# Splitting w_down into two parts with an accumulating DMA in place of a subtraction

## The chip, the cores and the metric

The kernel runs on one core of a Trainium2 chip. The time is the device time of one execution in microseconds (us). It is given as the median of three executions; one further execution was taken with the profiler, and every row quoted below is from that one.

## What is computed

Two layers of a hybrid block over a stream x (512 tokens, 1024 channels) and, in layer 0 alone, a context stream (256 tokens). What bears on the change is the feed-forward part at each layer's end:

```
D_FF = int(math.ceil(8 * D_MODEL / 3 / 128)) * 128      # 2816 = 22 blocks of 128
def conv_ffn(h, w_up, w_c, b_c, w_down):
    u = dwconv3(h @ w_up, w_c, b_c)
    gate, val = jnp.split(u, 2, axis=-1)
    return (jax.nn.silu(gate) * val) @ w_down
...
    yx = conv_ffn(fx, w_up[i], w_ffn_conv[i], b_ffn_conv[i], w_down[i])
    x = x + ga2 * rmsnorm(yx, g_post_ffn[i])
    if not last:
        yc = conv_ffn(fc, w_up[i], w_ffn_conv[i], b_ffn_conv[i], w_down[i])
```

## The kernel before

All products are made from rounded operands (fp32r). To keep fp32 accuracy each operand is split in two: a high part h, which is the value rounded to fp32r, and a low part, which is the value minus h. A product is then three matmuls (`mm3`, lines 196 to 198): high times high, high times low, low times high.

`load_w` fetches a block of 128 x 1024 weights (512 KB) into a tile Wr through SyncE's queue (line 189), and `split` makes the parts: ScalarE copies Wr to Wh, which rounds it (line 181), and VectorE or GpSimd writes Wl = Wr - Wh (line 182).

`ffn_down` needs one block of w_down for each of the 22 blocks m of D_FF. It is called for a group of two m at a time (the last call of the x stream has four) and multiplies the activations of the group before: gT for x, gc for the context. So w_down is loaded and split three times in all: for the context of layer 0 in `ffn_c` (22 blocks, split on GpSimd, since `CE` is True), for x of layer 0 in `ffn_x` (22, on VectorE) and for x of layer 1 (22, on VectorE). That makes 66 blocks.

In `ffn_x` the first half of the feed-forward product is a Strassen-like scheme of seven products for each m. Three more pairs of parts are made there for each m from w_up: from the raw block r, and from two tiles tt, which GpSimd makes with four subtractions (lines 1276 to 1279). A fourth, smaller pair is the tile w.

What sets the order:
- The pools. `BUFS` gives two buffers to Wr, four to Wh and four to Wl, and w_up and w_down share these. A new high or low part can only be written when the matmuls that read the old one in the same buffer are done.
- The scheduler. The build orders the instructions of each engine by a timeline of its own and by priority, which is the order of the code. The list so made is fixed; an engine then takes its instructions strictly in that order, and each waits for its own semaphores.
- The queues. SyncE issues all weight loads, GpSimd issues the DMAs of tables and spilled tiles, and both in their order.

Of the kernel before, what the change touches and what calls it, by code (L numbers as in the profile page):

```python
# [8 lines left out]
F32 = mybir.dt.float32  # L9
F32R = mybir.dt.float32r  # L10
I32 = mybir.dt.int32
AF = mybir.ActivationFunctionType
ALU = mybir.AluOpType
# [4 lines left out]
P = 128  # L18
# [50 lines left out]
class Net:  # L69
# [115 lines left out]
    def load_w(self, src, shape=None, el=None, tag=None, raw=None):  # L185
        shape = shape or [P, 1024]
        r = self.tl(shape, F32, raw or tag or "Wr")
        for i, a in enumerate(src if isinstance(src, list) else [src]):
            self.nc.sync.dma_start(r[:, 2 * i : 2 * i + 2] if isinstance(src, list) else r, a)
        h, lo = self.tl(shape, F32R, tag or "Wh"), self.tl(shape, F32R, tag or "Wl")  # L190
        self.split(h, lo, r, el)
        return h, lo

    def mm3(self, ps, l, r, first, last, **kw):
# [970 lines left out]
    def ffn_down(self, l, st, g, ms, begin, el=None, early=0, mid=None):  # L1165

        nc = self.nc
        end = ms[-1] == MF - 1
        if begin and st is self.X:
            st.y = [self.M("y", F32) for _ in range(st.NT)]  # L1170
        wd = {k: self.load_w(self.I["w_down"][l, k], el=nc.gpsimd if el else None) for k in ms}
        if end:
            ss = [self.small("ss", 2, 6) for _ in range(st.NT)]
            xr = [self.load_r(self.src[st.name][t]) for t in range(st.NT)]
        acc = {}

        def add(t, h, ks):
            hs, ts = slice(h * 512, (h + 1) * 512), slice(t * P, (t + 1) * P)
            if (t, h) not in acc:
                if h == 0:  # L1180
                    acc[t] = self.pw()
                acc[t, h] = acc[t][:, hs]
            for k in ks:
                self.mm3(acc[t, h], (g[k][:, 0, ts], g[k][:, 1, ts]), (wd[k][0][:, hs], wd[k][1][:, hs]), k == ms[0], k == ms[-1])
            yield 3 * len(ks) * C512, 0.0

        for t in range(early):
            for h in range(2):
                yield from add(t, h, ms[:-1])
        for t in range(st.NT):  # L1190
            y = st.y[t]
            for h in range(2):
                hs = slice(h * 512, (h + 1) * 512)
                yield from add(t, h, ms[-1:] if t < early else ms)
                if end:
                    nc.vector.tensor_tensor(y[:, hs], y[:, hs], acc[t, h], op=ALU.add)
                    self.sumsq_half(ss[t], y[:, hs], h)
                    nc.gpsimd.tensor_tensor(y[:, hs], y[:, hs], st.G[1][:, hs], op=ALU.mult)
            if begin:
                nc.scalar.copy(y, acc[t])  # L1200
            elif not end:
                nc.vector.tensor_tensor(y, y, acc[t], op=ALU.add)  # L1202
            else:
                self.tail(st, t, xr[t], ss[t])
                if t == Z["MT"] and mid:
                    yield from mid
# [495 lines left out]
```

## Time and profile before

| | before |
|---|---|
| median of three runs | 1789.37 us (1785.97 to 1790.05) |
| the profiled execution | 1784.91 us, of it 1783.1 us span |
| mean granted TensorE clock in it | 0.971 |
| context feed-forward, layer 0 | about 484 to 690 us of the span |
| x feed-forward, layer 0 | about 690 to 1092 us |
| x feed-forward, layer 1 | about 1420 to 1783 us |
| TensorE busy over the span | 1639.1 us, 92% |
| VectorE, ScalarE, GpSimd busy | 1440.1, 934.9, 692.3 us |

How to read it: the span runs from the first to the last instruction, and 1.8 us of the execution lie around it. PE is TensorE's matmul row, PEld its weight loads, DVE VectorE, ACT ScalarE, POOL GpSimd, SP SyncE. A busy PE does not mean a PE at its peak, since matmuls are pipelined; so the text also uses the pace at which matmuls start. The time of a DMA is that from the start of its issue to its landing.

### The profile page before, as it was taken

What the parts mean: (1) busy time and instruction counts of PE and PEld (TensorE: products, weight loads), DVE (VectorE), ACT (ScalarE), POOL (GpSimd) and SP (SyncE); (2) the same over time, 40 slices, a digit from 0 to 9 for tenths busy, and PEclk for the clock granted to TensorE, in tenths of its full rate; (3) what the DMA queues carried; (4) which work ended last, traced back from release to release, by engine and by line L of the source; (5) the groups of instructions that cost most, each with busy time, mean ns of one, the idle gap of its engine ahead of it and who ended that gap; (6) DMA issues with size and microseconds to landing.
All of it is one profiled execution on the core that took longest, in us unless ns stands there. A gap on an engine that the chain in (4) does not pass through costs nothing. (4 is left out here: it accounts for less than half of the span.)

```text
span 1783.1 us, 27842 instructions
## 1 busy us (share of the span) xinstructions
PE 1639.1 (92%) x10502; PEld 1397.4 (78%) x10502; DVE 1440.1 (81%) x2324; ACT 934.9 (52%) x1737; POOL 692.3 (39%) x515
## 2 busy tenths in 40 slices
PE   5799987899999997989999998998898799999997
PEld 2677775687788897878989885787787678889996
DVE  5888777697665688889988987668895878999997
ACT  2642344487565454556554556434773465555454
POOL 3343332000134337665554645212002455655543
PEclk9899999999999998999999999999999899999999
DMA  9214277603477642332342258653012343332323
GB/s 366 101 61 146 86 243 263 232 13 130 162 253 232 228 155 71 96 118 84 101 148 84 89 185 305 213 175 118 1 48 83 130 146 103 95 107 86 127 62 119
DMA packets 70003, 248.01 MB, mean 139 GB/s; under 512 B 8111, under 2 KB 9647, under 8 KB 69868
## 3 DMA queue, kind: packets, MB, share of 16 engines
q1 hardware_dynamic: 60716, 215.54, 35.6%
q0 software_dynamic: 9152, 30.68, 5.5%
q8 instruction: 83, 1.36, 0.3%
q14 instruction: 52, 0.43, 0.1%
HBM read 232.03 MB, written 14.16 MB: 138 GB/s over the span
## 5 line engine op out<-in xcount | busy, mean ns | idle before, releaser
L196 PE MATMUL pn<-h,Wh 128*128 128x256 f32 x1328 | 376.6, 286 | 11.7 <-DVE ft L638 4.3
L198 PE MATMUL pn<-h,Wl 128*128 128x256 f32 x1328 | 372.8, 284 | 10.2 <-DVE Wl L182 10.2
L197 PE MATMUL pn<-h,Wh 128*128 128x256 f32 x1328 | 374.2, 283 | 1.7 <-POOL h L182 1.7
L196 PEld LDWEIGHTS pn<-h,Wh 128*128 128x128 f32 x1328 | 253.2, 191 | 24.5 <-issue 7.8
L198 PEld LDWEIGHTS pn<-h,Wl 128*128 128x128 f32 x1328 | 252.1, 191 | 15.3 <-DVE Wl L182 12.7
L197 PEld LDWEIGHTS pn<-h,Wh 128*128 128x128 f32 x1328 | 253.8, 191 | 6.2 <-POOL h L182 2.4
L181 ACT CAST Wh<-Wr 128x1024 fp32r<-128x1024 f32 x118 | 122.7, 1049 | 138.9 <-PE pw L198 46.4
L182 DVE TENSOR_TENSOR Wl<-Wr,Wh 128x1024 fp32r<-128x1024 f32 x89 | 129.7, 1465 | 53.7 <-ACT Wh L181 53.2
L1276 POOL TENSOR_TENSOR tt<-r,r 128x512 f32<-128x512 f32 x44 | 75.0, 1705 | 233.9 <-DMA r<-w_up 211.0
L196 PE MATMUL pw<-Wh,gT 128*128 128x512 f32 x352 | 137.5, 404 | 9.0 <-ACT gT L181 3.9
L197 PE MATMUL pw<-Wl,gT 128*128 128x512 f32 x352 | 138.5, 396 | 3.1 <-DVE Wl L182 3.1
L198 PE MATMUL pw<-Wh,gT 128*128 128x512 f32 x352 | 137.8, 396 | 1.8 <-DVE gT L182 1.8
L181 ACT CAST Wh<-tt 128x1024 fp32r<-128x1024 f32 x88 | 90.8, 1048 | 84.9 <-PE pn L197 42.4
L182 DVE TENSOR_TENSOR Wl<-tt,Wh 128x1024 fp32r<-128x1024 f32 x88 | 122.5, 1411 | 11.0 <-ACT Wh L181 8.0
L1335 POOL TENSOR_TENSOR ft<-ft,ft 128x512 f32<-128x512 f32 x44 | 70.8, 1609 | 132.4 <-DVE ft L638 94.2
L1202 DVE TENSOR_TENSOR y<-y,pw 128x1024 f32<-128x1024 f32 x82 | 99.2, 1213 | 20.1 <-PE pw L198 20.0
L182 POOL TENSOR_TENSOR h<-tf,h 128x256 fp32r<-128x256 f32 (+1 forms) x40 | 36.0, 921 | 187.8 <-ACT h L181 186.5
L182 POOL TENSOR_TENSOR Wl<-Wr,Wh 128x1024 fp32r<-128x1024 f32 x29 | 74.6, 2578 | 57.7 <-ACT Wh L181 56.5
L1278 POOL TENSOR_TENSOR tt<-r,tt 128x512 f32<-128x512 f32 x44 | 75.8, 1722 | 51.9 <-DVE Wl L182 51.9
L196 PE MATMUL pw<-h,Wh 128*128 128x256 f32 (+1 forms) x224 | 76.9, 343 | 13.9 <-DVE v L638 2.6
L283 PE MATMUL pn<-wm,cpad 128*32 128x256 f32 x768 | 67.6, 411 | 19.7 <-DMA wm<-w_mod 19.3
L636 ACT ACTIVATE ft<-C,vec 128x512 f32<-128x512 f32 x88 | 68.7, 811 | 32.1 <-DVE C L1325 25.7
(361 smaller groups left out, 4706.1 us busy)
## 6 DMA issues: line engine op xcount, KB each, us to landing
wm<-w_mod SPq DMA_DIRECT2D x96, 512.0 KB, 5.4
r<-w_up SPq DMA_DIRECT2D x90, 512.0 KB, 3.6
Wr<-w_down SPq DMA_DIRECT2D x66, 512.0 KB, 3.8
L<-w_up SPq DMA_DIRECT2D x44, 512.0 KB, 4.4
Wr<-w_out SPq DMA_DIRECT2D x24, 512.0 KB, 3.6
Wr<-w_in_t SPq DMA_DIRECT2D x16, 512.0 KB, 3.9
dft<-hdft_x POOLq DMA_DIRECT2D x16, 512.0 KB, 4.1
Wr<-w_in_c SPq DMA_DIRECT2D x12, 512.0 KB, 3.6
```

Of the source, the lines that this page charges most:

```text
L181: r = nc.scalar.copy(hi, src)
L182: (el or nc.vector).tensor_tensor(lo, src, f32(hi), op=ALU.subtract)
L196: nc.tensor.matmul(ps, l[0], r[0], start=first, stop=False, **kw)
L197: nc.tensor.matmul(ps, l[0], r[1], start=False, stop=False, **kw)
L198: nc.tensor.matmul(ps, l[1], r[0], start=False, stop=last, **kw)
L283: nc.tensor.matmul(ps[32 * g : 32 * g + 32, cs], self.cpad[:, q % 2 * 4 + g, :], w[:, g, :], start=q % 2 == 0, stop=q % 2 == 1, skip_group ...
L636: nc.scalar.activation(dst, ps, AF.Identity, scale=w1, bias=b)
L1202: nc.vector.tensor_tensor(y, y, acc[t], op=ALU.add)
L1276: te.tensor_tensor(half(t13, 0), half(r[1], 0), half(r[0], 0), op=ALU.subtract)
L1278: te.tensor_tensor(half(t24, 0), half(r[1], 1), half(t13, 0), op=ALU.subtract)
L1335: nc.gpsimd.tensor_tensor(o[0], o[0], o[1], op=ALU.mult)
```

## The change

For w_down alone, `load_w` gives way to a new function. It still loads Wr through SyncE's queue and still copies Wr to Wh on ScalarE. The low tile is first filled by ScalarE with the negated Wr, rounded to fp32r, which is the negated high part. Then a DMA issued by GpSimd reads the same block of w_down from HBM a second time and adds it to what stands in Wl. The subtraction goes, on both engines, in all 66 blocks.

```diff
+    def load_w_acc(self, src):
+        nc = self.nc
+        r = self.tl([P, 1024], F32, "Wr")
+        nc.sync.dma_start(r, src)
+        h, lo = self.tl([P, 1024], F32R, "Wh"), self.tl([P, 1024], F32R, "Wl")
+        nc.scalar.activation(lo, r, AF.Copy, scale=-1.0)
+        nc.scalar.copy(h, r)
+        nc.gpsimd.dma_start(lo, src, accum_op=ALU.add)
+        return h, lo
...
-        wd = {k: self.load_w(self.I["w_down"][l, k], el=nc.gpsimd if el else None) for k in ms}
+        wd = {k: self.load_w_acc(self.I["w_down"][l, k]) for k in ms}
```

In the new code the copies stand in lines 200 (the negated one) and 201 (Wh) and the accumulating DMA in line 202; all later lines have moved by 11, so `mm3` is in lines 207 to 209, GpSimd's four subtractions in 1287 to 1290, and the multiplication of line 1335 in 1346.

The scheduler has laid the instructions out anew from the first w_down block on. One group of two blocks in the middle of layer 1's x feed-forward serves as the example. The first place is ScalarE. Before, the two roundings of w_down have one activation of the convolution between them:

```order
L1298 COPY C_15830<-pn_15831 128x256
L181 CAST Wh_15764<-Wr_15762 128x1024
L636 ACTIVATE ft_15749<-C_15626,vec_101 128x512
L181 CAST Wh_15770<-Wr_15768 128x1024
L181 CAST gT_15621<-ft_15613 128x512
```

Now four full passes over a block follow each other, and in each pair the high part comes ahead of the negated one, though the code has them the other way round:

```order
L1309 COPY C_15882<-pn_15883 128x256
L201 CAST Wh_15814<-Wr_15812 128x1024
L200 ACTIVATE Wl_15815<-Wr_15812 128x1024
L201 CAST Wh_15821<-Wr_15819 128x1024
L200 ACTIVATE Wl_15822<-Wr_15819 128x1024
L647 ACTIVATE ft_15799<-C_15676,vec_101 128x512
```

What moved: the convolution's activation stands behind all four passes, and the accumulating DMA of the first block has two passes ahead of it.

The second place is GpSimd's queue at the same group. Before, it holds only the four subtractions for the next m and the multiplications:

```order
L1276 TENSOR_TENSOR tt_15936<-r_15929,r_15928 128x512
L1277 TENSOR_TENSOR tt_15936<-r_15929 128x512
L1335 TENSOR_TENSOR ft_15613<-ft_15613,ft_15614 128x512
L1278 TENSOR_TENSOR tt_15937<-r_15929,tt_15936 128x512
L1279 TENSOR_TENSOR tt_15937<-tt_15937,r_15928 128x512
L1335 TENSOR_TENSOR ft_15749<-ft_15749,ft_15750 128x512
```

Now the two accumulating DMAs stand behind the four subtractions and ahead of a multiplication:

```order
L1288 TENSOR_TENSOR tt_15988<-r_15981 128x512
L1289 TENSOR_TENSOR tt_15989<-r_15981,tt_15988 128x512
L1290 TENSOR_TENSOR tt_15989<-tt_15989,r_15980 128x512
L202 DMA Wl_15815<-w_down 128x1024
L202 DMA Wl_15822<-w_down 128x1024
L1346 TENSOR_TENSOR ft_15799<-ft_15799,ft_15800 128x512
```

What moved: two DMA issues are new here, and each waits for ScalarE's negated copy with the multiplication queued behind it.

The third place is TensorE's first use of the low part. Before (Wl_15765):

```order
L198 MATMUL pn_15860<-h_14318,Wl_15741 128x256
L196 MATMUL pn_15860<-h_14318,Wh_15740 128x256
L197 MATMUL pw_15774<-Wl_15765,gT_15417 128x512
L198 MATMUL pw_15774<-Wh_15764,gT_15417 128x512
L197 MATMUL pw_15788<-Wl_15765,gT_15417 128x512
```

Now (Wl_15815):

```order
L208 MATMUL pn_15926<-h_14370,Wh_15788 128x256
L209 MATMUL pn_15926<-h_14369,Wl_15789 128x256
L208 MATMUL pw_15826<-Wl_15815,gT_15465 128x512
L209 MATMUL pw_15826<-Wh_15814,gT_15465 128x512
L207 MATMUL pw_15826<-Wh_15821,gT_15671 128x512
L208 MATMUL pw_15840<-Wl_15815,gT_15465 128x512
```

What moved: little. Between the last matmul that reads the old content of this buffer and the first that reads the new low part, there stand 40 matmuls of 256 columns and 2 of 512 columns; before, there were 44 and 2 at this group, and 38 and 2 at most groups of the layer. The first use of the second block's low part stands later than before: 10 us of matmuls behind the release of its buffer, against 6.

## The prediction

> **What bounds the kernel now.** I read first the busy time by stage (the view of windows), then TensorE's waits in the two x feed-forward stages, where 44 of the 66 blocks are split.
>
> ```profile
> core 0: us, PE busy (x) PEld busy (x) DVE busy (x) ACT busy (x) POOL busy (x), PEclk, DMA share, GB/s
> 484.00:690.00 206.00, 200.13 (x1457) 177.28 (x1456) 151.87 (x234) 111.21 (x173) 92.19 (x57) 0.98 0.61 205
> 690.00:1092.00 402.00, 379.40 (x2540) 340.59 (x2538) 348.70 (x440) 217.71 (x357) 223.57 (x144) 0.98 0.38 126
> 1420.00:1745.00 325.00, 314.17 (x2180) 287.39 (x2180) 290.60 (x319) 173.87 (x270) 169.70 (x103) 0.99 0.32 104
> ...
> PE pn L198 <- DVE Wl L182: 4.5, 6, 1.4
> PE pw L197 <- DVE Wl L182: 3.1, 2, 2.0
> PE pw L196 <- DVE y L1202: 2.6, 1, 2.6
> ...
> PE pw L198 <- DVE gT L182: 0.9, 1, 0.9
> ...
> PE pn L198 <- DVE Wl L182: 4.1, 3, 2.5
> ...
> PE pn L196 <- DVE C L1323: 1.1, 3, 0.7
> PE pw L198 <- DVE gT L182: 0.9, 1, 0.9
> ...
> PE pw L196 <- DVE y L1202: 0.7, 2, 0.4
> ```
>
> The three stages are bound by TensorE: it is busy 200 of 206, 379 of 402 and 314 of 325 us. VectorE, at 87 and 89%, is near, but not the bound. All of TensorE's idle time in the two x stages is 22.6 + 10.8 = 33.4 us. The rows of waits (the first four those of 690 to 1092 us, the rest those of 1420 to 1745) lay 11.1 + 6.8 = 17.9 us of it to VectorE, and only 3.1 us (pw L197) to a low part of the down product. That is all that a lighter VectorE can give back.
>
> **What is removed.** The subtractions: 22 blocks in each x stage on VectorE, and the context's on GpSimd.
>
> ```profile
> L182 DVE TENSOR_TENSOR Wl<-Wr,Wh 128x1024 fp32r<-128x1024 f32 x22 | 36.7, 1677 | 2.9 <-ACT Wh L181 2.9
> L182 DVE TENSOR_TENSOR Wl<-Wr,Wh 128x1024 fp32r<-128x1024 f32 x22 | 36.9, 1697 | 0.5 <-ACT Wh L181 0.4
> L182 POOL TENSOR_TENSOR Wl<-Wr,Wh 128x1024 fp32r<-128x1024 f32 x20 | 51.3, 2573 | 46.7 <-ACT Wh L181 46.5
> ```
>
> VectorE loses 73.6 us of work, GpSimd 51.3. Nearly all of it lies beside matmuls. Of the 17.9 us I credit a third, 6 us: the waits on gT, C and y are for work with other inputs, and only a part of them stems from VectorE's queue being full. In the context stage I credit nothing: TensorE waits there on no GpSimd row, and is 97% busy.
>
> **What is added.** 66 passes of ScalarE, 66 DMA issues on GpSimd, and 66 times 512 KB through the DMA engines.
>
> ```profile
> L181 ACT CAST Wh<-Wr 128x1024 fp32r<-128x1024 f32 x118 | 122.7, 1049 | 138.9 <-PE pw L198 46.4
> L716 POOL DMA_DIRECT2D dft<-hdft_x x16: 527/591/956, 79.7 to 1173.0; - x16
> Wr<-w_down SPq DMA_DIRECT2D x66, 512.0 KB, 3.8
> dft<-hdft_x POOLq DMA_DIRECT2D x16, 512.0 KB, 4.1
> DMA to landing us min/median/max: 8.3/11.1/14.1
> GB/s 13 16 203 340 258 307 311 332 392 410 416 419 416 419 383 400 410 416 406 397 410 413 419 419 410 89 92 318 279 292 367 272 288 200 13 190 275 56 301 416
> ```
>
> As work this is cheap: 66 x 1.05 = 69 us for a ScalarE that is about half busy in these stages (217.71 of 402), 66 x 0.59 = 39 us for GpSimd, less than it loses, and 34.6 MB for DMA engines that are at most 61% busy. Its cost is latency. A low part was ready one ScalarE pass and one subtraction after its buffer came free; now it takes two passes, an issue and a landing, and TensorE's order leaves no more room for that. Here is one group in the timeline before:
>
> ```profile
> 1547.62 1.06 ACT L181 CAST Wh<-Wr 128x1024 fp32r<-128x1024 f32 x1
> 1550.04 1.65 DVE L182 TENSOR_TENSOR Wl<-Wr,Wh 128x1024 fp32r<-128x1024 f32 x1
> 1551.71 4.27 SPq L189 DMA_DIRECT2D Wr<-w_down  x2
> 1552.06 0.28 PE L196 MATMUL pn<-h,Wh 128*128 128x256 f32 x1
> 1552.18 0.28 PE L197 MATMUL pn<-h,Wh 128*128 128x256 f32 x1
> 1552.89 0.40 PE L197 MATMUL pw<-Wl,gT 128*128 128x512 f32 x1
> 1553.12 0.40 PE L198 MATMUL pw<-Wh,gT 128*128 128x512 f32 x1
> 1542.47 2.17 POOL L1279 TENSOR_TENSOR tt<-tt,r 128x512 f32<-128x512 f32 x1
> 1548.36 2.24 POOL L1276 TENSOR_TENSOR tt<-r,r 128x512 f32<-128x512 f32 x1 [3.72 <-DVE Wl L182]
> ```
>
> ScalarE starts at 1547.6, as soon as the old matmuls are done; the subtraction ends at 1551.7, and TensorE reads the low part at 1552.9: 1.2 us to spare, no stall. Matmuls start every 0.118 us (256 columns, the rows of 1552.06 and 1552.18) or 0.235 us (512). In the new order 40 short and 2 long ones lie between the release and the first use: 40 x 0.118 + 2 x 0.235 = 5.2 us. Into this must go about 0.2 us to ScalarE's start, two passes of 1.05, 0.1 to the issue (both small times are my estimates from rows like these), and the landing time A of an accumulating DMA. So TensorE stalls A - 2.8 us in such a group.
>
> **The price of A.** No row shows an accumulating DMA. Lower bound: a plain 512 KB copy issued by GpSimd lands in 4.1 us. Far end: the rows "to landing" of h<-spill_h, GpSimd's four fp32-to-fp32r copies of 512 KB beside other loads, give 8.3 us for the fastest and 11.1 for the median. I take 4.1 plus two transfers of 512 KB at the 419 GB/s of a full slice, 1.25 us each: one because the old content of Wl has to be read as well, one because the negated copy that releases this DMA also frees Wr, so that SyncE's next load starts at the same moment (in the timeline it starts at 1551.71, where the subtraction ends). A = 6.6 us, nearer to the plain copy since only two transfers collide, not eight. The far ends stay for the range.
>
> In the Trainium skill, the page Collectives: The Full Stack, section "Why ReduceScatter is half of AllGather", says that the add in a DMA engine costs no time itself, but that it needs two source reads on one ring, which halves the rate. By that alone A would be 4.1 + 1.25 = 5.35 us and the stalls would add up to 35 us; no row here shows it.
>
> **The sum.** The room between a buffer's release and its first use, counted in the new order for each group and turned into time with the two paces, gives at A = 6.6: ten groups with 5.2 us of room (three at the end of layer 0, seven in layer 1) at 3.7, 37 us; one in layer 1 with 6.1 us, 2.8; one in layer 0 whose two blocks have only 2.8 and 6.3 us, 9.3 together; the other groups of the x stages, with 7 to 9 us, 9 in all; and nothing for layer 0's last four blocks (15 us and more) or the context's (10 to 19). That is 58 us. The second block of a group has 10 us of room and needs 2.1 us more than the first: no stall of its own. At A = 4.1 the same sum is 17 us, at 8.3 it is 111, at 11.1 it is 239.
>
> What is queued behind the new waits: on GpSimd the two issues wait for ScalarE until about 5 us after the release, and the multiplication L1346 stands behind them. Its result gT is first read a group (31 us of matmuls) later, so this costs nothing. ScalarE's two activations of the convolution are pushed back some 4 us; TensorE's next need of their banks falls in its own stall. GpSimd's four subtractions stand ahead of the issues and run at 1.3 to 2.2 us each; if they end late, A starts late, and this is part of why the range leans upward. Since every stall stands on TensorE, the bound, it goes fully into the time.
>
> Net: 58 - 6 = +52 us. The profiled execution, 1784.9, would become 1837. It lay 4.5 us under the median of the three runs, so against the median the forecast is 1789.4 + 52 = 1841 us. One measurement of this kernel can tell 0.2% (3.6 us) from no change.
>
> **Rivals.**
> 1. The accumulating DMA lands like a plain one, A = 4.1 (the row of dft speaks for it, the doubled read against it): 17 - 6 = +11, 1800 us. Chance 0.15.
> 2. VectorE's relief wins. If A is 3.8, as SyncE's w_down loads have it, the ten groups stall 0.9 us each and the others 4, 13 us, and if all 17.9 us of waits on VectorE went, the kernel would end at 1785; some more, since freed tt tiles let GpSimd start earlier, at 1775 to 1785. It decides below A of about 4.2. For it: VectorE is nearly 90% busy. Against it: TensorE waits little on it. Faster 0.11; no change within 0.2%, with A near 4, 0.09.
> 3. The add is much slower than a copy, or GpSimd's subtractions hold the issue back by 2 us and more: A of 8.3 and above, +105 us, 1894 us or more. For it: the slow h<-spill_h. Against it: those ran at full DMA load. Chance 0.17.
>
> The forecast itself, A between 4.5 and 8, has 0.48. So slower by over 0.2%: 0.48 + 0.15 + 0.17 = 0.80; same 0.09; faster 0.11. For 8 in 10 the range starts below rival 1 (1796) and ends at rival 3's near edge (1894).
>
> In the Trainium skill, DMA: Bandwidth & Descriptors, section "Issuing engines are not separate DMA queues", has DMAs of all issuing engines on the same 16 engines; the 11.1 us of h<-spill_h at full load agree. By it a move to GpSimd's queue alone buys no bandwidth.
>
> **What would show it.** The row of the accumulating DMAs should show 5.5 to 8 us to landing. TensorE's waits should have a new row at the down product (pw, the line of high times low, now 208) that waits for a DMA or for Wl, with ten and more waits of 2.5 to 5 us; VectorE should be 70 us less busy, ScalarE 69 us more, and the context stage as long as before. The prediction is wrong if A is about 4 us or less, if the stalls appear in the context stage too (then ScalarE or GpSimd's order is the cause), or if TensorE's idle time falls.

## The result, and the profile after

| | before | after |
|---|---|---|
| median | 1788.56 us (4 runs, 1785.97 to 1790.05) | 1940.65 us (4 runs, 1931.73 to 1948.43) |
| ratio | | 1.085, 95% interval 1.080 to 1.0901 |
| profiled span | 1783.1 us | 1936.4 us |
| mean granted TensorE clock | 0.971 | 0.931 |

The change costs 152 us. The forecast was +52 us with a range up to 1894, so it had the sign right, but the size is almost three times as large.

The first view is the busy time by stage, with the stages' new bounds:

```profile
core 0: us, PE busy (x) PEld busy (x) DVE busy (x) ACT busy (x) POOL busy (x), PEclk, DMA share, GB/s
484.00:705.00 221.00, 203.54 (x1456) 179.72 (x1455) 144.83 (x235) 130.19 (x196) 48.67 (x52) 0.98 0.80 241
705.00:1160.00 455.00, 389.52 (x2502) 350.02 (x2500) 310.78 (x389) 233.57 (x360) 222.55 (x165) 0.91 0.46 129
1507.00:1936.00 429.00, 365.59 (x2310) 328.91 (x2310) 283.62 (x350) 210.39 (x323) 197.75 (x135) 0.90 0.42 118
```

The third stage before, taken to its end like the one above:

```profile
1420.00:1783.00 363.00, 340.95 (x2307) 308.25 (x2306) 316.39 (x371) 187.78 (x300) 183.38 (x113) 0.98 0.32 106
```

TensorE is idle for 17, 65 and 63 us of these stages. Before, it was idle for 6, 23 and 22 us. The granted clock, 0.98 in both x stages before, is 0.91 and 0.90. VectorE got lighter, as the change meant it to, and that bought nothing. The waits of TensorE have one large new row. The first row below is that of the whole span; the three behind it are those of the context, of x in layer 0 and of x in layer 1. The columns are us in total, times, and the longest.

```profile
PE pw L208 <- DMA Wl<-w_down: 104.7, 31, 7.7
...
PE pw L208 <- DMA Wl<-w_down: 13.0, 8, 2.5
...
PE pw L208 <- DMA Wl<-w_down: 44.7, 12, 7.7
...
PE pw L208 <- DMA Wl<-w_down: 47.1, 11, 6.4
```

One group of layer 1 in the timeline (start, duration, engine) shows the mechanism:

```profile
1653.75 1.05 ACT L201 CAST Wh<-Wr 128x1024 fp32r<-128x1024 f32 x1 [1.62 <-PE pn L208]
1654.71 1.05 ACT L200 ACTIVATE Wl<-Wr 128x1024 fp32r<-128x1024 f32 x1
...
1656.11 0.88 POOL L202 DMA_DIRECT2D Wl<-w_down  x1
...
1655.79 2.23 SPq L198 DMA_DIRECT2D Wr<-w_down  x2
...
1658.73 0.28 PE L209 MATMUL pn<-h,Wl 128*128 128x256 f32 x1
1663.36 0.79 PE L208 MATMUL pw<-Wl,gT 128*128 128x512 f32 x1 [4.35 <-DMA Wl<-w_down]
...
1666.09 0.41 PE L207 MATMUL pn<-h,Wh 128*128 128x256 f32 x1
1666.30 0.41 PE L208 MATMUL pn<-h,Wh 128*128 128x256 f32 x1
...
1668.34 0.28 PE L208 MATMUL pn<-h,Wh 128*128 128x256 f32 x1
1668.46 0.28 PE L209 MATMUL pn<-h,Wl 128*128 128x256 f32 x1
```

Up to 1663.36 this is the forecast, step by step, with a somewhat longer stall than the 3.7 us of the sum. ScalarE starts at 1653.75 and makes two passes, SyncE's next load starts at the moment the negated copy ends, GpSimd issues at 1656.11, and 7.25 us later TensorE goes on, after a stall of 4.35 us. But look at the four matmuls behind the stall. Those at 1666.09 and 1666.30 start 0.21 us apart, and the same kind at 1668.34 and 1668.46 starts 0.12 us apart. The view of windows shows why (ahead of the stall, behind it, and later; the third number from the end is the granted clock):

```profile
1630.00:1661.00 31.00, 29.01 (x202) 26.88 (x201) 24.74 (x29) 17.34 (x26) 16.90 (x11) 0.99 0.30 81
1661.50:1668.00 6.50, 4.64 (x15) 4.06 (x16) 0.82 (x1) 1.14 (x2) 1.94 (x1) 0.50 0.88 246
1668.50:1690.00 21.50, 21.50 (x146) 19.66 (x145) 19.75 (x21) 10.00 (x15) 11.52 (x7) 1.00 0.25 74
```

The stall is followed by several us at a granted clock of 0.50. That term is not in my sum at all. Short stalls cost less of it: in the context stage, where the longest wait is 2.5 us, the mean clock stays at 0.98.

How the 152 us divide was worked out from the starts of the three-part matmuls (8100 in the whole run, some 6700 of them from the context stage's first low part on, which are those used). An interval of more than 2.3 times the pace at full clock is counted as a stall; what a shorter one has over that pace is counted as slow pace. Stalls went from 236.6 to 350.6 us (+114), slow pace from 29.3 to 65.6 us (+36).

### The profile page after: what moved, and what is told of

It reads as the page before. It is cut to its first block, busy times and chain, and to the rows that moved or that the text cites. A ratio compares the mean times of both kernels' runs of the same rounds, so it can differ in the third digit from the quotient of the medians.

```text
span 1936.4 us, 27997 instructions
## 1 busy us (share of the span) xinstructions
PE 1692.3 (87%) x10502; PEld 1440.3 (74%) x10502; DVE 1371.8 (71%) x2280; ACT 997.7 (52%) x1803; POOL 667.4 (34%) x559
## 5 line engine op out<-in xcount | busy, mean ns | idle before, releaser
L207 PE MATMUL pn<-h,Wh 128*128 128x256 f32 x1328 | 385.0, 293 | 13.8 <-ACT Wh L181 8.2
L208 PE MATMUL pn<-h,Wh 128*128 128x256 f32 x1328 | 381.8, 290 | 1.9 <-POOL h L182 1.9
L207 PEld LDWEIGHTS pn<-h,Wh 128*128 128x128 f32 x1328 | 264.1, 199 | 26.4 <-ACT Wh L181 11.4
L208 PEld LDWEIGHTS pn<-h,Wh 128*128 128x128 f32 x1328 | 264.1, 199 | 6.9 <-POOL h L182 2.5
L208 PE MATMUL pw<-Wl,gT 128*128 128x512 f32 x352 | 151.7, 431 | 87.2 <-DMA Wl<-w_down 87.2
L207 PE MATMUL pw<-Wh,gT 128*128 128x512 f32 x352 | 147.3, 428 | 5.2 <-ACT Wh L201 2.9
L208 PEld LDWEIGHTS pw<-Wl,gT 128*128 128x128 f32 x352 | 71.1, 202 | 107.5 <-DMA Wl<-w_down 93.1
L209 PE MATMUL pw<-Wh,gT 128*128 128x512 f32 x352 | 147.6, 420 | 0.0
L182 DVE TENSOR_TENSOR Wl<-tt,Wh 128x1024 fp32r<-128x1024 f32 x88 | 131.0, 1506 | 16.1 <-ACT Wh L181 16.0
L648 DVE SCALAR_TENSOR_TENSOR ft<-C,vec,ft 128x511 f32<-128x511 f32 x88 | 89.9, 1049 | 54.7 <-ACT ft L647 54.7
L1213 DVE TENSOR_TENSOR y<-y,pw 128x1024 f32<-128x1024 f32 x82 | 99.4, 1213 | 39.3 <-PE pw L209 39.2
L202 POOL DMA_DIRECT2D Wl<-w_down x66 | 60.3, 920 | 136.2 <-ACT Wl L200 88.6
L181 ACT CAST Wh<-Wr 128x1024 fp32r<-128x1024 f32 x52 | 54.3, 1050 | 86.7 <-PE pw L209 45.4
L182 DVE TENSOR_TENSOR Wl<-Wr,Wh 128x1024 fp32r<-128x1024 f32 x45 | 56.1, 1249 | 51.7 <-ACT Wh L181 51.4
```

Of the source, the lines that this page charges most:

```text
L181: r = nc.scalar.copy(hi, src)
L182: (el or nc.vector).tensor_tensor(lo, src, f32(hi), op=ALU.subtract)
L202: nc.gpsimd.dma_start(lo, src, accum_op=ALU.add)
L207: nc.tensor.matmul(ps, l[0], r[0], start=first, stop=False, **kw)
L208: nc.tensor.matmul(ps, l[0], r[1], start=False, stop=False, **kw)
L209: nc.tensor.matmul(ps, l[1], r[0], start=False, stop=last, **kw)
```

## The experiments

All times are medians; ratios are to the kernel before, run on the same chip, with a 95% interval. Of the forecasts that follow, those of e_none, e_copy (rival A3), b_late, c_ltx and b_ltt held. e_add, e_ctx, e_fill, e_late, e_late_x and c_lt came out 2, 7, 6, 23, 21 and 6 us above the upper end of theory A; e_tt came out 31 us below its range, and b_tt 41 below its own.

| kernel | us | ratio |
|---|---|---|
| e_none, no DMA | 1788.73 | 0.9996 (0.9981 to 1.001) |
| e_add, an addition in place of the DMA | 1801.61 | 1.0072 (1.0048 to 1.0096) |
| e_copy, a plain DMA | 1840.13 | 1.0288 (1.0256 to 1.0319) |
| e_ctx, context alone | 1822.08 | 1.0179 (1.0157 to 1.0201) |
| e_fill, stalls filled with work | 1936.29 | 1.0819 (1.0788 to 1.0849) |
| e_late, low parts used later | 1888.15 | 1.0553 (1.0534 to 1.0573) |
| e_late_x, the same, x alone | 1860.52 | 1.0404 (1.0379 to 1.0429) |
| e_tt, tt on VectorE | 1873.52 | 1.0466 (1.0417 to 1.0515) |
| c_lt, e_late and e_tt | 1845.73 | 1.0334 (1.0307 to 1.036) |
| c_ltx, the same, x alone | 1812.96 | 1.0144 (1.0119 to 1.0169) |
| c_ltxh, and Wh by VectorE | 1829.36 | 1.0233 (1.0208 to 1.0257) |
| b_late, before with e_late's order | 1798.62 | 1.0058 (1.0037 to 1.0079) |
| b_tt, before with tt on VectorE | 1758.93 | 0.9846 (0.9822 to 0.9871) |
| b_ltt, before with both | 1766.02 | 0.9885 (0.9862 to 0.9908) |

**What the DMA costs, and what the add in it costs: e_none, e_copy, e_add**

```diff
-        nc.gpsimd.dma_start(lo, src, accum_op=ALU.add)
e_copy:
+        nc.gpsimd.dma_start(lo, src)
e_add (VectorE for x, GpSimd for the context):
+        (el or nc.vector).tensor_tensor(lo, f32(lo), r, op=ALU.add)
```

> The changed kernel with the accumulating DMA left out: the low part is the negated high part, so the down product is without its low term's value; all matmuls and both ScalarE passes stay, neither a DMA nor a subtraction is issued. It measures the term that my sum credited with 6 us, VectorE's and GpSimd's relief, without the landing. Theory A: 1775 to 1795 us (e_add, which still has an addition, had 1802; the relief by my reading of the waits is 6 to 18 us). If the relief were worth as much as VectorE's 74 us of work: 1740 us or less. If ScalarE's pass were the cost: above 1800 us.

> The changed kernel, with the accumulating DMA replaced by an in-place addition Wl = Wl + Wr on the engine that did the subtraction before. ScalarE's extra pass and the chain of two engines stay, the DMA and the second read go. Theory A (the time is lost to the landing of the DMA, by TensorE's stalls and the half clock after them): 1785 to 1800 us, TensorE's idle time in the two x stages near the 33 us of before, granted clock 0.97. Rival B (the extra ScalarE pass, or the order that the scheduler made anew, costs the time): 1850 us or more.

> The changed kernel, with the DMA a plain copy into Wl in place of an accumulating one (the low part then holds the whole weight, so the result is not the block's). Same order, same issues, same chain. Theory A1 (the add halves the rate of the packets, 328 ns for 4 KB, and the rest of the landing is latency of the queue): packets of 160 to 200 ns, landing 1.3 us shorter, stalls 31 x 1.3 = 40 us shorter, 1885 to 1905 us. Rival A2 (the add itself is free, latency is all): no shorter, 1930 to 1945 us. Rival A3 (the add makes the issue and the start dear too): landing near the 4.1 us of a plain copy, 1840 to 1860 us.

Without the DMA (and with the low term's value left out) the changed kernel takes as long as the one before. So ScalarE's 66 extra passes cost, together with what VectorE and GpSimd gain, nothing. The +152 us come with the DMA: a plain copy has 51 of it (1840 - 1789), the add the other 101 (1941 - 1840). The two parts are not equally clean. In the traces e_copy has the same instructions in the same order as the changed kernel on TensorE, VectorE, ScalarE and GpSimd, so that the 101 us are the add's alone. e_none was laid out anew by the scheduler, so that the 51 us hold the copy's landing together with the order that goes with it. In the waits of e_copy's TensorE 43.5 us stand for w_down:

```profile
PE pw L208 <- DMA Wl<-w_down: 43.5, 19, 5.5
```

e_add, with an addition on the engine, was 2 us past theory A's upper end; rival B is out. For the copy the rival A3 was right and not A1: I had weighed the add by its packets alone. GpSimd's DMAs go through one queue, and the page's part on queues gives its packets, MB and share of 16 engines' span. The changed kernel:

```profile
q0 software_dynamic: 18656, 65.29, 14.5%
```

e_copy, and the kernel before:

```profile
q0 software_dynamic: 18656, 65.29, 10.8%
```

```profile
q0 software_dynamic: 9152, 30.68, 5.5%
```

Each share times 16 and the span, less that of before, over the 9504 packets that came in: 308 ns for an accumulating packet against 170 ns for a plain one, a factor of 1.8 (short packets at the end of each DMA included; those of 4 KB alone take 328 and 174 ns at the median in layer 1's x stage). The Trainium skill's Collectives: The Full Stack, section "Why ReduceScatter is half of AllGather", has the add read two sources on one ring and halve the rate; the packets agree with that, but the estimate of 5.35 us that the prediction worked out by it fell short, since the landing grew by more than one transfer at full rate. Issue to landing in layer 1's x stage, of the changed kernel:

```profile
DMA to landing us min/median/max: 6.4/8.8/12.1
```

and of e_copy:

```profile
DMA to landing us min/median/max: 4.5/5.9/9.5
```

The fastest differ by 1.9 us and the medians by 2.9, where eight packets per engine at 0.14 us more give 1.1. GpSimd is busy 0.87 us with an accumulating issue against 0.58 with the copy, at the median. The packets' own times show more: in four steady groups of layer 1 (those issued at 1618.6, 1656.1, 1693.9 and 1809.7 us) the first DMA's first 4 KB packet starts 2.3 to 2.7 us after the issue, against 2.4 in the same groups of e_copy, and from the first of its 128 to the last it takes 3.1 to 4.3 us against 1.6 to 1.8. So it is the stream of packets, beside SyncE's load, that got longer, and not the start. A group's two DMAs follow each other on one queue: the second is issued 1.9 us after the first, and in these four groups its packets start only when the first's have all started, 6.7 to 7.1 us after the first issue. In six of the eight steady groups of layer 1 e_copy stalls for 1.6 to 1.8 us, with 4.5 to 4.8 us from issue to first use; "A - 2.8" of the prediction gives 1.7 to 2.0. With the add, six of eight groups had 6.5 to 7.2 us. So the formula holds at two values of A.

**The context: e_ctx**

```diff
+        wd = {k: self.load_w_acc(...) if el else self.load_w(...) for k in ms}
```

> Only the context's 22 blocks of w_down use the accumulating DMA, the 44 of x are split as before. My prediction gave the context stage no cost: 1785 to 1792 us. Theory A from the trace of the changed kernel, where the matmuls of the context stage wait some 1 to 3.4 us in ten places: +15 to +25 us, 1804 to 1815 us.

+33 us, where I had put nothing. TensorE's waits in the context stage, in e_ctx:

```profile
PE pw L208 <- DMA Wl<-w_down: 10.6, 10, 1.8
```

and in e_copy, all there are:

```profile
PE pn L209 <- DVE Wl L182: 3.0, 1, 3.0
PE pn L294 <- DMA wm<-w_mod: 2.9, 1, 2.9
```

With a plain copy in the changed kernel's order no wait for w_down is left there (the first row's Wl is a subtraction's), where the changed kernel waits 13.0 us. So it is not ScalarE's or GpSimd's order alone, which the prediction named for this case. What I had not counted is that the landing is longer where more is being loaded. The DMA engines are at 0.80 in this stage of the changed kernel, and e_ctx's DMAs took 7.1, 9.4 and 11.4 us at the least, the median and the most. By the prediction's own sum (A and 2.4 us for passes and issue) a landing of 9.4 needs 11.8 us, more than the 10 of the tightest groups. By the starts of the same matmuls before and after, 15 to 21 us of the lag had come by the end of the context's main part. The rest came in x of layer 0, where the context's last group is run and where e_add, too, lost some 10 us; what makes that part is not settled.

**The half clock: e_fill**

```diff
+            for i in range(16 if el is None and (t, h) == (0, 0) and ks[0] == ms[0] else 0):
+                nc.tensor.matmul(acc[t, h], g[ks[0]][:, 0, ts], wd[ks[0]][0][:, hs], start=True, stop=True)
             for k in ks:
                 self.mm3(...)
```

> The changed kernel with 16 matmuls of 512 columns added (high part times high part, overwritten by the real product's start) ahead of each x group's first product of the down projection: 16 x 0.235 = 3.8 us of useless work, 20 times 3.8 = 75 us in all, in the place where TensorE otherwise stalls for the low part. Theory A (the stall itself halves the granted clock for the 6.8 us that follow): the work fits into the stalls of most groups, costs some 10 to 15 us where the stall was shorter, and the clock stays up, which gives back up to 35 us: 1910 to 1930 us, faster than the changed kernel although it does more, granted clock 0.96 to 0.97. Rival (the half clock has nothing to do with the stalls): clock 0.93 as before, 1945 to 1960 us.

75 us of useless matmuls on the engine that is the bound cost nothing: 1936.3 against 1940.7. Some 52 of the 75 took the place of stalls; the other 23 were paid by the clock. The clock came back, as theory A said, though the time is 6 us above its range. The changed kernel's clock was 0.931. The clock of e_fill, and its waits for Wl:

```profile
core 0: 1930.5 us, clock 0.962
```

```profile
PE pw L208 <- DMA Wl<-w_down: 62.9, 33, 6.4
```

Slow pace fell from 65.6 to 35.8 us, near the 29.3 of before; the stalls, less the 75 of filling, from 350.6 to 299 us. Since only work in the place of the stalls was added, the stalls are what lowers the clock, and about 30 us of the 152 are due to it. The Trainium skill's TensorE: Matmul & The Clock Gate, section "HAM oscillation — how this bites in real kernels", describes just this, a clock that falls to half after a wait for a DMA. The trace agrees, with 0.50 behind the stall of 4.35 us. I had read that clock as 0.98 before and had left it there.

**The queue: e_tt, with b_tt as its control**

```diff
-        te = nc.gpsimd
+        te = nc.vector
```

> The changed kernel, with the four subtractions that make tt moved from GpSimd to VectorE, so that nothing but the multiplication stands ahead of the accumulating DMAs on GpSimd's queue in the x stages. Theory A with the queue as a term: the issues that followed ScalarE's negated copy by 2 to 6 us in eight groups (about 30 us together) follow it by 0.3 us, 1905 to 1925 us. Rival (the late issues don't matter, or VectorE, which takes 176 more instructions, becomes the bound): 1940 us or more.

> Control: the kernel before with tt made on VectorE, no accumulating DMA. VectorE would take on 176 instructions of 0.74 us (130 us) in stages where it is 87 to 89% busy, and become the bound unless its other instructions get faster by as much, as they did in e_tt (the first taps of the convolution 0.77 in place of 1.05 us): 1800 to 1840 us. If it is no slower than before, a part of what e_tt gained has nothing to do with the DMA's queue.

In the changed kernel some issues come late, since the subtractions of tt stand ahead of them. This group is in layer 0:

```profile
853.10 1.05 ACT L200 ACTIVATE Wl<-Wr 128x1024 fp32r<-128x1024 f32 x1
...
854.74 2.35 POOL L1287 TENSOR_TENSOR tt<-r,r 128x512 f32<-128x512 f32 x1 [4.81 <-DVE ft L649]
857.05 1.31 POOL L1288 TENSOR_TENSOR tt<-r 128x512 f32<-128x512 f32 x1
858.31 1.74 POOL L1289 TENSOR_TENSOR tt<-r,tt 128x512 f32<-128x512 f32 x1
860.00 0.87 POOL L202 DMA_DIRECT2D Wl<-w_down  x1
```

ScalarE is done at 854.2, GpSimd issues at 860.0. In e_tt nearly all issues follow ScalarE by 0.3 us, and the kernel is 67 us faster than the changed one. But its control is faster as well: the kernel before gains 30 us by the same edit, where I had expected a loss. What is left for the queue is the difference: the accumulating DMA costs 152 us with the subtractions on GpSimd and 115 (1873.5 - 1758.9) without, so 37 us. This number is not sharp, since e_tt's runs lie between 1860 and 1881 us, and it is not all seen in the trace. The waits of e_tt for Wl, and its landings:

```profile
PE pw L208 <- DMA Wl<-w_down: 90.1, 37, 7.6
DMA to landing us min/median/max: 6.3/9.4/13.7
```

The waits fell by only 15 us, from 104.7. Five first DMAs of layer 0 that the changed kernel issues 2 to 6 us behind ScalarE land in 5.2 to 6.1 us (a sixth, in the stage's last group, in 10.0); in e_tt none of the 66 lands in less than 6.3. By these landings an issue that comes earlier gives a part of its gain back, and what makes up the rest of the 37 is open.

**Hiding the landing: e_late, e_late_x, b_late, c_lt, c_ltx, c_ltxh, b_ltt**

All products with Wh of the first two token tiles come ahead of those with Wl (n runs over the three kinds of product):

```diff
+            for n in range(3):
+                for t in tiles:
...
+                            gi, wi = ((0, 0), (1, 0), (0, 1))[n]
+                            nc.tensor.matmul(acc[t, h], g[k][:, gi, ts], wd[k][wi][:, hs], ...)
```

> The changed kernel, with the products of the first two token tiles of each x group written in another order: all products with the high part of w_down first, those with the low part last. The sums are the same, no instruction is added; 14 more matmuls of 512 columns stand ahead of the first use of the low part, 14 x 0.235 = 3.3 us of useful work in the place of the stall. Theory A (landing against room, and the half clock behind each stall): steady stalls go from about 4 to below 1 us, the sum of the waits for Wl falls from 105 to 30 to 50 us, granted clock 0.95 to 0.965, 1830 to 1865 us. Rival (DMA load or the second read slows TensorE's work as a whole): 1920 us or more.

> The kernel of e_late, with the context's 22 blocks split as before by GpSimd's subtraction. Theory A: the context's 20 to 30 us (e_ctx measured 33) come off e_late: 1800 to 1840 us; below 1789 us only if VectorE's relief is worth more than what is left of the stalls. A rival by which the context's cost was only moved from the x stages: no more than 5 us below e_late.

> Control: the kernel before with the order of products of e_late, no accumulating DMA. Theory A: its low part was in time already, 1785 to 1800 us. If the order by itself were worth a lot, below 1780 us.

> e_late and e_tt together: low parts used last in the first two token tiles of each x group, and tt made on VectorE, so that no subtraction stands ahead of the DMAs on GpSimd. Theory A (landing, queue and room add up, so the two cures act on different terms): e_late took 52 us off the changed kernel and e_tt 67; together 100 to 119 less, 1820 to 1840 us, waits for Wl in the x stages below 15 us, clock 0.965. If both cured the same microseconds: 1865 to 1875 us.

> c_lt with the context's blocks split as before. Theory A: e_late_x stood 28 us below e_late, so 25 to 30 us below c_lt, 1792 to 1815 us. Whether it beats the kernel before depends on what VectorE's relief is worth: not below 1785 us by my reading of the waits before.

> c_ltx with the high part of the x blocks' w_down written by VectorE in place of ScalarE, so that one ScalarE pass, not two, stands ahead of each accumulating DMA. Theory A: the DMA starts 1 us earlier; 5 to 15 us below c_ltx where stalls are left. Rival: VectorE's 44 further passes come on a full engine, the same or up to 10 us above c_ltx.

> Control for c_ltx: the kernel before with tt on VectorE and with the order of products of e_late, no accumulating DMA. If the two edits add up as they did alone (b_tt -30, b_late +8): 1764 to 1772 us, and the 44 x blocks' DMAs still cost c_ltx some 45 us. If c_ltx's loss were the two edits' own doing: 1800 us or more.

e_late took 52 us off, but less than I expected. The order by itself is no gain: in b_late it costs the kernel before some 8 us. The waits of e_late for Wl, in the reordered and in the other products:

```profile
PE pw L1210 <- DMA Wl<-w_down: 38.8, 17, 3.9
...
PE pw L208 <- DMA Wl<-w_down: 18.8, 15, 2.6
```

Those of c_ltx:

```profile
PE pw L1210 <- DMA Wl<-w_down: 25.9, 24, 2.6
...
PE pw L208 <- DMA Wl<-w_down: 8.3, 5, 2.8
```

The room was gained, and in places the queue took a part of it back: in the group at 1626 us ScalarE is done at 1625.8 and the issue waits behind two subtractions until 1627.5. With the queue cleared too (c_lt) the time falls by 95 us in all, not by the 119 of both alone. c_ltx leaves the context out and is 33 us below c_lt, as e_ctx had it. It still loses 47 us to its control b_ltt, which has the same two edits without the DMA. Its waits above hold 34 of these 47, in 29 places with a landing of 8.6 us at the median; the others I can't place. c_ltxh went the rival's way and past it, 16 us above c_ltx. Its waits for the low part grew by 5 us, to 39.2, and those for the high part that VectorE now writes are 2.2 us; where the rest went is not traced.

So no form of the change that I tried comes out ahead. Two kernels beat the one before, and neither has anything of the change: b_tt with 1758.93 us, 1.5% below it, and b_ltt with 1766.02.

## Why the prediction was wrong, point by point

- **What bounds the kernel.** Right. TensorE was the bound in all three stages, and VectorE's load was no limit; it fell by 68 us (1440.1 to 1371.8), and ScalarE's rose by 63, near the 70 and 69 of the forecast. The credit of 6 us is measured by e_none as nothing (ratio 0.9996), together with ScalarE's passes.
- **The chain and the price A.** Right for a group by itself: 6.6 us forecast, 6.5 to 7.2 in six of layer 1's eight steady groups, stalls of 3.6 to 4.4 against 3.7 in five of them (A - 2.8 at 6.6 is 3.8, so the sum is about 1 us short there). Its two parts of 1.25 us each were not both right, and the fit is in part luck: e_copy has the collision with SyncE's load without the add and lands in 4.5 to 4.7 us, 0.4 to 0.6 above the plain 4.1, and the add brings some 2 us. Too small as a value for all: 8.9 and 9.3 in the other two, and a median of 9.2 over all 66. A group's second DMA, which the first holds up, is slow in that median; the firsts alone have 8.4, and 9.3 in the context. The step that failed is "two transfers collide, not eight". By the packets, SyncE's queue moved 0.5 to 1.0 MB while the first DMA landed in the six groups that fit, less than two blocks of 512 KB, and 1.1 to 2.5 MB in the ten pairs of the context's main part, two blocks to five.
- **The sum of stalls.** 58 us forecast, 104.7 in the row of waits and 114 by the matmuls' starts. 13 of it are in the context, where the sum had nothing; 44.7 in layer 0, where it had about 25; 47.1 in layer 1 against about 33.
- **GpSimd's subtractions ahead of the issues.** Named, but priced at nothing in the sum: 37 us by the pair of controls, of which the waits for Wl show 15.
- **What a stall leaves behind.** "Since every stall stands on TensorE, the bound, it goes fully into the time": it goes in with more than itself, slow pace +36 us, of which e_fill gave back 30.
- **The rivals.** The outcome is the third, add much slower than a copy and issues held back, to which I gave 0.17 and whose near edge (1894) I took as the end of the range. Its argument against itself, that the slow h<-spill_h copies "ran at full DMA load", overlooked that the context stage runs at a DMA share of 0.8 once the second read is added.

The terms overlap, so they do not add up to the total as they stand: 115 + 37 = 152 is one cut (with and without the subtractions on GpSimd), 51 + 101 another (copy and add), 114 + 36 a third (stalls and clock).

## What to carry to other kernels

A DMA in the place of an engine's pass takes its work from an engine and puts its latency on a chain. Before the trade, compare that latency with the room between a buffer's release and its next reader, with a value for each stage's DMA load and not one for all. Count a stall of several us of the bounding TensorE at more than its length, since here the half clock behind it cost again. And run the control of every cure on the kernel before: the best result here came from one.

## What the runs showed of the hardware that I had not expected

VectorE got slower here by what GpSimd did beside it. In b_tt VectorE has 176 instructions more, yet its busy time rose only from 1440.1 to 1444.3 us. Groups of the kernel before (count, busy time, mean ns of one):

```profile
L182 DVE TENSOR_TENSOR Wl<-Wr,Wh 128x1024 fp32r<-128x1024 f32 x89 | 129.7, 1465 | 53.7 <-ACT Wh L181 53.2
...
L637 DVE SCALAR_TENSOR_TENSOR ft<-C,vec,ft 128x511 f32<-128x511 f32 x88 | 81.3, 945 | 2.2 <-ACT ft L636 2.2
...
L1202 DVE TENSOR_TENSOR y<-y,pw 128x1024 f32<-128x1024 f32 x82 | 99.2, 1213 | 20.1 <-PE pw L198 20.0
```

The first of tt's subtractions there, on GpSimd, in the view of the tile (least, median and most ns):

```profile
L1276 POOL TENSOR_TENSOR tt<-r,r x44: 1285/1606/3049, 687.0 to 1723.2; 128x512 f32<-128x512 f32 x44
```

Groups of b_tt:

```profile
L182 DVE TENSOR_TENSOR Wl<-Wr,Wh 128x1024 fp32r<-128x1024 f32 x89 | 112.1, 1261 | 56.4 <-ACT Wh L181 56.0
...
L637 DVE SCALAR_TENSOR_TENSOR ft<-C,vec,ft 128x511 f32<-128x511 f32 x88 | 65.8, 754 | 0.1
...
L1202 DVE TENSOR_TENSOR y<-y,pw 128x1024 f32<-128x1024 f32 x82 | 99.5, 1216 | 21.5 <-PE pw L198 21.4
...
L1276 DVE TENSOR_TENSOR tt<-r,r 128x512 f32<-128x512 f32 x44 | 32.9, 748 | 8.5 <-DMA r<-w_up 8.4
```

Instructions with two operands in SBUF fell from 1465 to 1261 and from 945 to 754 ns, while the one that reads PSUM (y, pw) stayed at 1213 and 1216. A subtraction of tt takes 0.75 us on VectorE against 1.6 on GpSimd. The Trainium skill's SBUF — State Buffer, section "Who interferes with whom", says that a VectorE instruction with two SBUF inputs contends with a GpSimd one that reads SBUF; the rows agree, the unchanged one of y included. By that rule a part of VectorE's busy time, 87 and 89% in the x stages, is waiting for a port; and the work moved onto it came at almost no cost in its busy time. How the 30 us of b_tt come about is not shown by this alone: by the starts of the matmuls, worked out as above, its stalls are 17 us and its slow pace 12 us below those of the kernel before.
